# A two-layer diffusion trunk on one core: where PSUM changes hands around the MLPs, and a first stage that prepares two tiles ahead

## The chip, the cores and the metric

One core of a Trainium2 chip runs the whole program. The metric is the device time of one execution in microseconds; the kernel before took 1693.77 us in the median of three runs (1693.08 to 1694.43).

## What is computed

640 rows (512 latent, 128 context) of width 1024 pass two layers. Each has a mixer (differential attention, then neighbourhood attention) and a squared-ReLU MLP of width 4096; each half scales and shifts its input, multiplies its output by a gate and ends in a LayerNorm. Shift, scale and gate are columns of a modulation product. All in fp32.

```python
def modulate(x, shift, scale):
    return x * (1 + scale) + shift

def sq_relu_mlp(h, w1, w2):
    return jnp.square(jax.nn.relu(h @ w1)) @ w2

for i in range(DEPTH):
    mp = modulation(c_ctx, w_mod[i], b_mod[i])
    ...
    y, state = ctx_mixers[m](modulate(xp, mp[0], mp[1]), *params[i])
    xp = layer_norm(ALPHA * xp + mp[2] * y, ln_g[i, 0], ln_b[i, 0])
    y = sq_relu_mlp(modulate(xp, mp[3], mp[4]), w_mlp1[i], w_mlp2[i])
    xp = layer_norm(ALPHA * xp + mp[5] * y, ln_g[i, 1], ln_b[i, 1])
    ... # the same for the latent rows xs
```

## The kernel before

Every fp32 product is made of three matmuls: each operand is split into a high part (a cast, `hhi`, `wh`, `uhi`) and a low part (the difference, `hlo`, `wl`, `ulo`), and `mm3` (lines 120 to 122) adds high x high, low x high and high x low. So TensorE does three passes, ScalarE makes the high parts (L127 for activations, L195 for weights) and VectorE the low ones (L128, L197); with `pool_lo` above zero some low parts of weights go to GpSimd instead. Raw weights `rw` come through SP's DMA queue.

TensorE's instructions run in the order in which the program is written; the order on ScalarE, VectorE, GpSimd and SP is a scheduler's. PSUM has eight banks. `banks(kind, m)` closes the pools in use and opens others: two S tiles or O tiles in up to four banks, and `m` banks for M tiles (128 x 512). A tile of a new pool takes banks of the old one, so its first matmul waits until the old tile there has been read.

The places that the change touches, in order of time:

- `start` (0 to 57 us). Per tile of 128 input columns: modulation matmuls (L260), a copy and a transposition (L269), `mod_affine` (VectorE: `red`, `mc`, `AB`), scaling of `x` (L417), split, and `main`, 15 matmuls of 512 columns. Preparation of tile g stands around `main(g - 1)`.
- `rest` (the MLP of layer l; 443 to 905 us and 1247 us to the end). The up projection comes in four groups `gr` of two chunks c with four tiles f each. In group 0, chunk 0, the columns up to 256 were multiplied earlier (`first`, in S and O tiles); `act` squares them (ScalarE relu L1198, VectorE L1199, split L127 and L128), then `banks(None, 6)`, then the four tiles' columns from 256 on (M tiles of 384 columns). `act_ctx` squares the 128 context rows as `rc`, which are transposed on TensorE (L1217) after the next tile. `next(mods)` puts a step of the next layer's modulation columns on VectorE (L294, `jk`).
- The last down projection (`down`). For layer 0 `banks("S", 4)` stands ahead of it. Then, by `ORDER_LN`, n (down projection of a row tile, second half, with LayerNorm L1010 to L1020), h (transposition of the tile to h, L1060) and v (first value columns of layer 1) follow each other.

## Time and profile before

| | |
|---|---|
| median of 3 runs | 1693.77 us (1693.08 to 1694.43) |
| the profiled execution | 1694.21 us |
| its span | 1692.4 us |
| TensorE busy | 1611.3 us, 95% |
| VectorE, ScalarE, GpSimd busy | 65%, 40%, 19% |
| DMA, mean over the span | 119 GB/s |

Times in the rows are microseconds from the span's start. A matmul's duration in a row overlaps the next one's; how fast they follow is read from their starts. In brackets at a row's end stands how long the engine was idle before it, and which instruction it then waited for.

### The profile page before, as it was taken

Reading aid. Unit: us, or ns where it says so; the run is one execution under the profiler, and the core shown is the slowest. Engines: PE = TensorE matmul, PEld = TensorE weight load, DVE = VectorE, ACT = ScalarE, POOL = GpSimd, SP = SyncE. Lnnn points to the kernel's source line nnn. Section 1 sums busy time; section 2 is a strip of 40 time slices with the busy share of each in tenths; the row PEclk is TensorE's granted clock in tenths of the full one; section 3 lists DMA queues with packets and bytes.
Section 4 is the critical chain, followed back from the end, with each engine's and each line's share of the span. In section 5 each row is a group of like instructions: output and inputs, shape, how many; then the busy total and the mean of one; then the engine's idle time right before and its main releaser. Section 6 shows DMA issues by size and latency. Waiting matters only on the chain. (4 is left out here: it accounts for less than half of the span.)

```text
span 1692.4 us, 23972 instructions
## 1 busy us (share of the span) xinstructions
PE 1611.3 (95%) x9074; PEld 1394.7 (82%) x9074; DVE 1098.9 (65%) x2169; ACT 669.0 (40%) x1366; POOL 316.4 (19%) x260
## 2 busy tenths in 40 slices
PE   8999999899799999999999999998889999999997
PEld 5788889787788788778788999997788888888886
DVE  4788778875569979796365777778655543232337
ACT  2456555743531322312235555565452132131321
POOL 2100000000002236254211001100000224334321
PEclk9999999999899999999999999999999999999999
DMA  8442334331334545452224443444033122221211
GB/s 336 130 136 91 102 116 151 103 129 52 124 113 137 199 149 187 162 172 103 75 75 161 126 127 119 148 140 165 14 112 113 63 99 75 76 98 51 100 51 63
DMA packets 61367, 200.62 MB, mean 119 GB/s; under 512 B 7765, under 2 KB 14403, under 8 KB 60227
## 3 DMA queue, kind: packets, MB, share of 16 engines
q1 hardware_dynamic: 55618, 175.09, 30.3%
q0 software_dynamic: 5632, 23.99, 4.1%
q8 instruction: 72, 1.18, 0.3%
q14 instruction: 45, 0.36, 0.1%
HBM read 186.41 MB, written 7.40 MB: 115 GB/s over the span
## 5 line engine op out<-in xcount | busy, mean ns | idle before, releaser
L195 ACT CAST wh<-rw 128x1024 fp32r<-128x1024 f32 x192 | 200.2, 1053 | 380.1 <-PE M L122 287.9
L197 DVE TENSOR_TENSOR wl<-rw,wh 128x512 fp32r<-128x512 f32 x278 | 216.1, 811 | 128.7 <-ACT wh L195 128.0
L120 PE MATMUL M<-hhi,wh 128*128 128x512 f32 (+2 forms) x768 | 279.0, 363 | 8.1 <-DVE r L1199 7.9
L122 PE MATMUL M<-hhi,wl 128*128 128x512 f32 (+2 forms) x768 | 277.5, 361 | 1.8 <-DVE wl L197 1.8
L121 PE MATMUL M<-hlo,wh 128*128 128x512 f32 (+2 forms) x768 | 277.1, 361 | 0.0
L120 PE MATMUL M<-wh,uhi 128*128 128x512 f32 x640 | 250.9, 392 | 3.1 <-DVE rc L1199 3.1
L120 PE MATMUL M<-wh,hhi 128*128 128x256 f32 (+1 forms) x752 | 244.6, 325 | 8.7 <-DVE tmp L1143 3.2
L122 PE MATMUL M<-wh,ulo 128*128 128x512 f32 x640 | 249.9, 391 | 1.6 <-DVE ulo L128 1.6
L121 PE MATMUL M<-wl,uhi 128*128 128x512 f32 x640 | 249.9, 390 | 0.0
L197 POOL TENSOR_TENSOR wl<-rw,wh 128x512 fp32r<-128x512 f32 x106 | 181.9, 1726 | 345.0 <-ACT wh L195 344.7
L122 PE MATMUL M<-wh,hlo 128*128 128x256 f32 (+1 forms) x752 | 240.1, 319 | 5.0 <-DVE hlo L128 5.0
L121 PE MATMUL M<-wl,hhi 128*128 128x256 f32 (+1 forms) x752 | 239.5, 319 | 0.0
L120 PEld LDWEIGHTS M<-hhi,wh 128*128 128x128 f32 x768 | 146.1, 190 | 26.1 <-issue 8.2
L122 PEld LDWEIGHTS M<-hhi,wl 128*128 128x128 f32 x768 | 145.9, 190 | 20.8 <-DVE wl L197 3.3
L120 PEld LDWEIGHTS M<-wh,hhi 128*128 128x128 f32 x752 | 145.2, 193 | 20.6 <-DVE tmp L1143 3.4
L121 PEld LDWEIGHTS M<-hlo,wh 128*128 128x128 f32 x768 | 146.0, 190 | 17.2
L122 PEld LDWEIGHTS M<-wh,hlo 128*128 128x128 f32 x752 | 144.8, 193 | 17.9 <-DVE hlo L128 9.1
L121 PEld LDWEIGHTS M<-wl,hhi 128*128 128x128 f32 x752 | 145.2, 193 | 8.7
L120 PEld LDWEIGHTS M<-wh,uhi 128*128 128x128 f32 x640 | 120.5, 188 | 28.3 <-issue 3.5
L294 DVE SCALAR_TENSOR_TENSOR jk<-wm,cb 128x1024 bf16<-128x1024 f32 x96 | 141.7, 1476 | 2.9 <-DMA wm<-in_wmodT 1.9
L122 PEld LDWEIGHTS M<-wh,ulo 128*128 128x128 f32 x640 | 120.6, 188 | 27.7 <-DVE ulo L128 2.4
L121 PEld LDWEIGHTS M<-wl,uhi 128*128 128x128 f32 x640 | 120.6, 188 | 25.1 <-DVE wl L197 0.4
(284 smaller groups left out, 2459.9 us busy)
## 6 DMA issues: line engine op xcount, KB each, us to landing
rw<-in_w SPq DMA_DIRECT2D x192, 512.0 KB, 3.8
wm<-in_wmodT SPq DMA_DIRECT2D x48, 512.0 KB, 3.5
rw<-in_wmod SPq DMA_DIRECT2D x32, 512.0 KB, 4.5
E<-in_bias POOLq DMA_DIRECT2D x32, 384.0 KB, 5.2
wm<-in_wmod SPq DMA_DIRECT2D x8, 1024.0 KB, 10.8
Q<-Q SPq DMA_DIRECT2D x16, 320.0 KB, 3.8
gate<-gates POOLq DMA_DIRECT2D x6, 512.0 KB, 5.1
X<-in_xT SPq DMA_DIRECT2D x8, 320.0 KB, 11.4
```

Source lines behind the costliest of these rows:

```text
L120: te.matmul(out, sh, mh, start=start, stop=False)
L121: te.matmul(out, sh, ml, start=False, stop=False)
L122: te.matmul(out, sl, mh, start=False, stop=stop)
L195: keep(nc.scalar.copy(hi, r))
L197: keep(eng.tensor_tensor(lo[:, k], r[:, k], hi[:, k], ALU.subtract))
L294: op = nc.vector.scalar_tensor_tensor(jk, ws[t], 1.0, cb[:, x, :], ALU.mult, ALU.mult, accum_out=mc[:, t, x : x + 1])
```

## The change

Four edits. (1) `start` loads three tiles ahead, does the modulation, scaling and split of two tiles ahead of the first `main`, then two rounds ahead, and `pool_lo` is 0, so that VectorE makes all low parts. (2) In the MLP, `banks(None, 6)` moves from ahead of the first chunk to behind it; in layer 1 a `banks("S", 4)` stands ahead of the chunk. `banks("S", 4)` ahead of the last down projection of layer 0 is gone, and v takes M tiles, two to a bank. (3) `next(mods)` moves from `square` to `aside`, behind the split, and no longer follows the context squares; the transpositions of the context rows come after the second tile of a chunk. (4) `ORDER_LN` has v0 ahead of h3 and v2 ahead of h4.

```diff
-ORDER_LN = "n0 n1 h0 n2 h1 n3 h2 n4 h3 v0 v1 h4 v2 v3"
+ORDER_LN = "n0 n1 h0 n2 h1 n3 h2 n4 v0 h3 v1 v2 h4 v3"
...
-        self.pool_lo = 2
+        self.pool_lo = 0
...
+            for g in range(3):
+                load(g)
+            mod(0)
+            self.conv(0, False)
+            affine(0)
+            mod(1)
+            affine(1)
+            for g in range(KT - 1):
+                load(g + 3)
+                main(g, (0, 1))
+                if g == 0:
+                    main(g, (2, 3, 4))
+                mod(g + 2)
+                if g % 2:
+                    self.conv(g // 2 + 1, False)
...
+                if g:
+                    main(g, (2, 3, 4))
+                affine(g + 2)
             main(KT - 1, range(NTT))
...
             def square(r, src):
                 nc.scalar.activation(r, src, AF.Relu)
-                op = nc.vector.scalar_tensor_tensor(r, src, 0.0, r, ALU.max, ALU.mult)
-                if not quiet:
-                    next(mods, None)
-                return op
+                return nc.vector.scalar_tensor_tensor(r, src, 0.0, r, ALU.max, ALU.mult)
...
-            def aside(op):
+            def aside(op, x=0):
+                if gr and x < 2:
+                    next(mods, None)
...
                             act(us, f, first[f], slice(0, CUT))
-                        self.banks(None, 6)
+                        if l == 1:
+                            self.banks("S", 4)
                         for f in range(4):
                             m = self.M()[:, : NT - CUT]
                             self.ff(n, f, CUT, NT, m)
                             act(us, f, m, slice(CUT, NT))
+                        self.banks(None, 6)
...
                         aside(act(us, 4 * c + f, m, slice(0, NL)))
-                        while wait:
-                            wait.pop()()
+                    while wait:
+                        wait.pop()()
...
                 if t % 2 == 0:
-                    box.append(self.S())
-                m = box[-1][:, 512 * (t % 2) :]
-                self.nat(hT, t, NCH, m[:, :256], 0, 256)
+                    box.append(self.M())
+                m = box[-1][:, 256 * (t % 2) : 256 * (t % 2) + 256]
+                self.nat(hT, t, NCH, m, 0, 256)
...
             g, b = self.ln_tiles(pool, l, 1)
-            if l == 0:
-                self.banks("S", 4)
```

The functions `load`, `mod` and `affine` hold what stood in the loop of `start`: the DMA of a tile's weights and inputs (the first tile's weights in two halves); the modulation matmuls and the copy of their rows; the transposition, `mod_affine`, the scaling and the split.

TensorE at the entry of the first MLP, before: the last matmul of another S tile, the first of the first chunk (M_5274), the last of the fourth (M_5364), and the tile that follows (M_5431).

```order
L122 MATMUL S_5093<-hhi,wl_4998 128x256
L120 MATMUL M_5274<-hhi,wh_4831 128x384 [waits DVE_49,PE_49]
...
L122 MATMUL M_5364<-hhi,wl_4998 128x384
L120 MATMUL M_5431<-hhi,wh_5034 128x512
L121 MATMUL M_5431<-hlo,wh_5034 128x512
```

The same place in the changed kernel (M_5265, M_5355, M_5427), and the first matmul of the same chunk in the second MLP (M_12365).

```order
L122 MATMUL S_5089<-hhi,wl_4994 128x256
L120 MATMUL M_5265<-hhi,wh_4827 128x384 [waits Activation_49]
L121 MATMUL M_5265<-hlo,wh_4827 128x384 [waits DVE_49]
...
L122 MATMUL M_5355<-hhi,wl_4994 128x384
L120 MATMUL M_5427<-hhi,wh_5030 128x512 [waits DVE_49]
...
L120 MATMUL M_12365<-hhi,wh_12093 128x384 [waits DVE_49,PE_49]
```

The wait for VectorE (in both kernels for a square of a tile that held the bank) has moved from the first chunk to the tile behind the fourth; the first chunk waits only for the high and low parts of the last h tile. In the second MLP the first chunk waits for a square as before, and so does the tile behind its fourth.

VectorE in the third group of the first MLP, before: the square of the fourth tile (r_7017), two products of the modulation columns (jk), the low part of the square (ulo) and the square of the context rows (rc).

```order
L1199 SCALAR_TENSOR_TENSOR r_7017<-M_6917,r_7017 128x512 [waits Activation_49]
L294 SCALAR_TENSOR_TENSOR jk_7020,mc_103<-wm_6912,cb 128x1024 [waits DMAHW1_49,DVE_49]
L197 TENSOR_TENSOR wl_7035<-rw_6942,wh_7034 128x512 [waits DMAHW2_49,Activation_49]
L294 SCALAR_TENSOR_TENSOR jk_7022,mc_103<-wm_6912,cb 128x1024 [waits DVE_49]
L128 TENSOR_TENSOR ulo_6843<-r_7017,uhi_6842 128x512 [waits Activation_49]
L1199 SCALAR_TENSOR_TENSOR rc_7041<-M_6918,rc_7041 128x512 [waits Activation_49]
```

The same place in the changed kernel.

```order
L1218 SCALAR_TENSOR_TENSOR r_7001<-M_6901,r_7001 128x512 [waits Activation_49]
L197 TENSOR_TENSOR wl_7019<-rw_6926,wh_7018 128x512 [waits DMAHW1_49,Activation_49]
L128 TENSOR_TENSOR ulo_6827<-r_7001,uhi_6826 128x512 [waits Activation_49]
L294 SCALAR_TENSOR_TENSOR jk_7006,mc_103<-wm_6898,cb 128x1024 [waits DMAHW0_49]
L1218 SCALAR_TENSOR_TENSOR rc_7025<-M_6902,rc_7025 128x512 [waits Activation_49]
L294 SCALAR_TENSOR_TENSOR jk_7008,mc_103<-wm_6898,cb 128x1024 [waits DVE_49]
```

The products have moved behind the low part, the second of them behind the context square too.

TensorE from the end of layer 0 into layer 1, before: the last of v1 (in S_8533), h4's transpositions (L1060), the first of v2 (S_8606), the last of v3, and the first q/k matmul of layer 1 (M_8686).

```order
L122 MATMUL S_8533<-wh_8477,hlo 128x256
L1060 MATMUL M_8582<-idf,X_4337 128x128 [waits DVE_49,Pool_49]
...
L120 MATMUL S_8606<-wh_8213,hhi 128x256
...
L122 MATMUL S_8606<-wh_8477,hlo 128x256
L120 MATMUL M_8686<-hhi,wh_8213 128x320 [waits PE_49,Activation_49]
L121 MATMUL M_8686<-hlo,wh_8213 128x320 [waits DVE_49]
```

The same place in the changed kernel (v2 and v3 in M_8571, q/k in M_8674).

```order
L122 MATMUL M_8571<-wh_8466,hlo 128x256
L1081 MATMUL M_8596<-idf,X_4333 128x128 [waits DVE_49,Pool_49]
...
L120 MATMUL M_8571<-wh_8202,hhi 128x256 [waits Activation_49]
...
L122 MATMUL M_8571<-wh_8466,hlo 128x256
L120 MATMUL M_8674<-hhi,wh_8202 128x320 [waits DVE_49,PE_49]
```

One v more stands ahead of h4's transpositions, one less behind; the v's are M tiles, and the first q/k matmul waits for VectorE, for the split of a v whose bank it takes.

## Rows read from the trace of the kernel before

**Rows 1.** The page's first part: busy time, share of the span and instructions.
```profile
PE 1611.3 (95%) x9074; PEld 1394.7 (82%) x9074; DVE 1098.9 (65%) x2169; ACT 669.0 (40%) x1366; POOL 316.4 (19%) x260
```

**Rows 2.** TensorE's waits: for whom, us in total, times, longest.
```profile
PE M L120 <- DVE r L1199: 7.9, 2, 4.3
...
PE S L120 <- ACT hhi L127: 4.3, 5, 1.2
...
PE M L1060 <- DVE X L1020: 3.7, 1, 3.7
...
PE M L120 <- DVE rc L1199: 3.1, 1, 3.1
...
PE M L1217 <- DVE rc L1199: 2.3, 2, 1.2
PE M L120 <- DVE red L271: 2.2, 1, 2.2
...
PE M L122 <- DVE ulo L128: 1.6, 2, 0.8
```

**Rows 3.** Stretches: length, busy (PE, PEld, DVE, ACT, POOL), granted clock, DMA share, GB/s.
```profile
447.00:453.80 6.80, 5.89 (x18) 5.92 (x19) 2.72 (x7) 2.14 (x6) 2.28 (x5) 0.50 1.00 347
540.00:740.00 200.00, 194.60 (x860) 159.31 (x859) 175.98 (x234) 53.26 (x68) 76.01 (x42) 1.00 0.50 171
836.10:839.50 3.40, 3.40 (x10) 2.62 (x9) 0.00 (x0) 0.00 (x0) 0.00 (x0) 0.50 0.47 154
900.00:917.00 17.00, 13.30 (x87) 13.13 (x87) 8.69 (x16) 7.41 (x19) 4.10 (x8) 0.80 0.50 180
904.40:911.20 6.80, 5.71 (x27) 5.74 (x28) 2.12 (x3) 4.04 (x10) 0.00 (x0) 0.50 0.39 148
960.00:985.00 25.00, 20.79 (x154) 20.03 (x153) 20.78 (x58) 17.65 (x44) 4.05 (x8) 1.00 0.47 156
1249.10:1256.00 6.90, 5.83 (x18) 5.87 (x19) 1.20 (x4) 0.84 (x3) 0.00 (x0) 0.51 0.70 259
```

**Rows 4.** First stage: VectorE and GpSimd in time, then 20 to 57 us.
```profile
17.53 0.17 DVE L332 TENSOR_SCALAR AB<-mc 128x2 f32<-128x2 f32 x1
...
23.03 1.22 DVE L332 TENSOR_SCALAR AB<-mc 128x2 f32<-128x2 f32 x1
...
21.68 2.54 POOL L197 TENSOR_TENSOR wl<-rw,wh 128x512 fp32r<-128x512 f32 x2 [8.82 <-ACT wh L195]
...
20.00:57.00 37.00, 33.48 (x205) 22.55 (x202) 21.82 (x46) 13.35 (x22) 10.18 (x8) 1.00 0.62 239
```

**Rows 5.** Entry of the first MLP, in time: start, us, engine, what.
```profile
443.14 0.69 DVE L128 TENSOR_TENSOR hlo<-hs,hhi 128x512 fp32r<-128x512 f32 x1 [1.57 <-ACT hhi L127]
...
447.91 0.66 PE L120 MATMUL M<-hhi,wh 128*128 128x384 f32 x1 [4.30 <-DVE r L1199]
...
467.35 0.39 PE L120 MATMUL M<-hhi,wh 128*128 128x512 f32 x1
```

**Rows 6.** The fourth chunk's square: ScalarE, then VectorE, in time.
```profile
467.61 0.49 ACT L1198 ACTIVATE r<-M 128x384 f32<-128x384 f32 x1
...
466.41 3.09 DVE L197 TENSOR_TENSOR wl<-rw,wh 128x512 fp32r<-128x512 f32 x5
469.43 0.55 DVE L1199 SCALAR_TENSOR_TENSOR r<-M,r 128x384 f32<-128x384 f32 x1
```

**Rows 7.** Third group of the first MLP: VectorE's product, TensorE's wait.
```profile
724.36 1.21 DVE L294 SCALAR_TENSOR_TENSOR jk<-wm,cb 128x1024 bf16<-128x1024 f32 x1
...
726.24 0.50 PE L122 MATMUL M<-wh,ulo 128*128 128x512 f32 x1 [0.79 <-DVE ulo L128]
```

**Rows 8.** Layer 1's start: first q/k matmul, last split of V.
```profile
914.72 0.31 PE L120 MATMUL M<-hhi,wh 128*128 128x320 f32 x1
...
916.19 0.42 DVE L128 TENSOR_TENSOR V<-S,V 128x256 fp32r<-128x256 f32 x1 [0.44 <-ACT V L127]
```

**Rows 9.** The fourth chunk's square in the second MLP.
```profile
1271.65 0.55 DVE L1199 SCALAR_TENSOR_TENSOR r<-M,r 128x384 f32<-128x384 f32 x1
```

More of the change, by code (lines that the diff above doesn't have):

```diff
@@ L384, in start, with load @@
                 nc.tensor.matmul(warm[:, :P], self.idf, self.ones, start=True, stop=True)
-            for g in range(KT):
-                w = pool.tile([P, 2, 4, 256], F32, tag="wm0", name=self.nm("wm"), bufs=4)
-                nc.sync.dma_start(w, a["wmod"][g])
-                nc.sync.dma_start(x[:, g, :], a["xT"][:, g, :])
-                if g % 2 == 0:
-                    self.pump()
-                acc = self.M()
-                self.mod_mm(acc, w[:, 0], 0)
-                self.mod_mm(acc, w[:, 1], 1)
-                rows = pool.tile([P, 256], F32, tag="rows", name=self.nm("rows"), bufs=2)
-                self.tc.keep_in_program_order(nc.scalar.copy(rows, acc[:, :256]))
-                if g % 2 == 0:
-                    self.conv(g // 2, False)
+            ws, rows = {}, {}
+            def load(g):
+                if g < KT:
+                    ws[g] = pool.tile([P, 2, 4, 256], F32, tag="wm0", name=self.nm("wm"), bufs=4)
+                    for r in (slice(0, 1), slice(1, 2)) if g == 0 else (slice(0, 2),):
+                        nc.sync.dma_start(ws[g][:, r], a["wmod"][g][:, r])
+                    if g == 2:
+                        self.pump()
+                    nc.sync.dma_start(x[:, g, :], a["xT"][:, g, :])
+                    if g == 0 or g == 4 or g == 6:
+                        self.pump()
                 if g == KT - 1:
@@ L404, in start, with mod, affine @@
                     nc.sync.dma_start(self.bm[1], a["bmodT"][1])
+            def mod(g):
+                if g < KT:
+                    acc = self.M()
+                    self.mod_mm(acc, ws[g][:, 0], 0)
+                    self.mod_mm(acc, ws[g][:, 1], 1)
+                    rows[g] = pool.tile([P, 256], F32, tag="rows", name=self.nm("rows"), bufs=2)
+                    self.tc.keep_in_program_order(nc.scalar.copy(rows[g], acc[:, :256]))
+            def affine(g):
+                if g < KT:
+                    self.mod_T(rows[g], g)
+                    self.mod_affine(0, 0, g)
+                    for t, c in enumerate((slice(0, NL), slice(NL, NT))):
+                        nc.vector.tensor_scalar(
+                            x[:, g, c], x[:, g, c], A[:, 0, g, t : t + 1], mc[:, g, t : t + 1], ALU.mult, ALU.add
+                        )
+                    self.split(h[0][:, g, :], h[1][:, g, :], x[:, g, :])
+            for g in range(3):
[13 more added lines that the diff above has]
+                    self.conv(g // 2 + 1, False)
+                if g == KT - 2:
                     self.pin = True
@@ L407, in start @@
                     self.ready += 1
-                if g > 0:
-                    main(g - 1, (0, 1))
-                self.mod_T(rows, g)
-                if g > 0:
-                    main(g - 1, (2, 3, 4))
-                self.mod_affine(0, 0, g)
-                cuts = (0, 256, NL, NT) if g == KT - 1 else (0, NL, NT)
-                for c0, c1 in zip(cuts, cuts[1:]):
-                    t, c = c0 // NL, slice(c0, c1)
-                    nc.vector.tensor_scalar(
-                        x[:, g, c], x[:, g, c], A[:, 0, g, t : t + 1], mc[:, g, t : t + 1], ALU.mult, ALU.add
-                    )
-                    if g == KT - 1:
-                        self.split(h[0][:, g, c], h[1][:, g, c], x[:, g, c])
-                if g < KT - 1:
-                    self.split(h[0][:, g, :], h[1][:, g, :], x[:, g, :])
+                if g:
+                    main(g, (2, 3, 4))
+                affine(g + 2)
             main(KT - 1, range(NTT))
@@ L1250, in rest @@
                         continue
-                    quiet = gr == 0
                     for f in range(2):
@@ L1264, in rest @@
                         if k == 3:
-                            aside(act(us, 4 * c + 2 + x, ms[x], slice(0, NL)) if x < 2 else act_ctx(us, c, ms[x]))
+                            aside(act(us, 4 * c + 2 + x, ms[x], slice(0, NL)) if x < 2 else act_ctx(us, c, ms[x]), x)
                 if gr < 3:
```

1 line of the change is left out of this document (removed).

## The prediction, made before the changed kernel had run

> **What bounds the kernel now.** I read the page's first part first: TensorE is busy for 1611.3 of 1692.4 us and VectorE for 65% of it [rows 1]. TensorE is the bound, its work is not changed by one matmul, and so the change can only be worth what TensorE waits, and what it runs slowly after waiting. Next the list of its waits, longest in total first [rows 2]: it is a list of single events with a place each, and six of the seven lines shown belong to places that the diff touches. Last the granted clock by stretches [rows 3]: behind each wait of over 3 us that matters here the clock stands at 0.50, which is the lower of its two levels (1.2 GHz of 2.4), while 540 to 740, with two waits of 0.8 and two of 1.2 us in it, has 1.00 on the whole. A stretch of 3.4 us at half speed puts TensorE back by 1.7 us; so a wait that goes is worth itself plus half of the slow stretch behind it, and a wait that comes costs the same. The profiled execution took 1694.21 us, 1.8 us more than its span and 0.4 us more than the median of 1693.77 us; the sum is made against 1694.2 and 0.4 is taken off at the end.
>
> **First stage.** Its loop works tile by tile: modulation matmuls, a transposition, scaling on VectorE, a split, 15 matmuls. Every second round GpSimd makes two low parts (2.54 us) beside VectorE's scaling, and a tiny operation of VectorE, 0.17 us alone, then takes 1.22 us [rows 4]; TensorE waits for the split, five times in all, 4.3 us [rows 2]. The change prepares two tiles ahead and gives the low parts to VectorE. TensorE has 33.48 us of work between 20 and 57 us, so 3.5 us is idle there [rows 4]. With a lead of a whole round (about 4.5 us) over a chain of some 3 us, I count that idle as gone: **+3.5 us**. VectorE takes over the low parts, at 0.62 us each (five in 3.09 us, [rows 6]), 1.24 us a pair against GpSimd's 2.54; it is busy for 21.8 of those 37 us [rows 4], so there is room. The bounds: the five waits and the smaller ones give at most 5; if the first main matmuls come later, because the second tile's modulation now stands ahead of them, 1. The loads are issued three tiles ahead on SP's queue; their sum is the same, and what they push back are weights of the next chunk, needed only after 50 us.
>
> **Entry of the first MLP.** The first four chunks (columns from 256, 96 matmuls) get their bank today from the squares of the 256-column part: TensorE stands for 4.30 us until 447.91 [rows 5] and then runs at half speed to 453.8. In the changed kernel the first chunk writes a bank of the old pool. What it waits for is the last h tile: its low part is ready at 443.83 [rows 5], the second half of it before TensorE gets there. Start at 443.9 instead of 447.9 is 4.0, and 5.9 us at half speed, no longer there, is 2.9: **+6.9 us**. But the new pool now opens directly behind the fourth chunk, and the matmul that follows takes bank 2, which holds until VectorE has squared a tile of the fourth chunk. Today nobody waits for that: TensorE goes on at 467.35 [rows 5], ScalarE's relu of the chunk comes at 467.61, since two casts stand ahead of it, VectorE's square at 469.43, behind five low parts (3.09 us), and is done at 469.98 [rows 6]. The order of both engines there is the same after the change. So TensorE stands from the chunk's end, 467.4 in today's time, to about 469.9: **-2.5 us**. Behind that wait stand the whole second half of the first group's up projection. Net +4.4; bounds +1 (with 6.8 us at half speed behind the wait, as at 447) and +6.9 (if the square comes early).
>
> **Does the clock fall behind 2.5 us?** The rows leave it open: waits of 3.1 and more were followed by a fall, waits of up to 1.2 were not [rows 2, 3]. There will be two such waits (the second MLP has the other), and I count one fall of 3.4 us: **-1.7 us**. The Trainium skill, page TensorE: Matmul & The Clock Gate, section "A second HAM failure mode: psum-queue depth-cycling", says that short idles between groups, where a kernel cycles through PSUM banks, can be enough to make the clock swing. By that both waits would bring a fall and the sum would be 1.7 us less; the stretch from 540 to 740, which has such short idles at 1.00 [rows 3], speaks against it.
>
> **Middle of the first MLP.** VectorE computes the modulation columns of the next layer (1.21 us a product, [rows 7]) between a square and its low part; twice TensorE waits 0.79 us for that low part [rows 7], in all 1.6 us [rows 2]. The new order has the low part ahead of the product: gone. The transpositions of the context rows come after the second tile instead of the first; they wait 1.17 us twice today (2.3 us, [rows 2]) for a square that is queued behind products on VectorE. A tile is 24 matmuls of 0.23 us (860 in 194.6 us, [rows 3]), 5.5 us of cover: gone. **+3.9 us** together. The products that no longer follow the context squares move into the last group; VectorE is busy for 176 of 200 us in the middle [rows 3], so a new short wait of about a microsecond is possible; bounds +2 and +3.9.
>
> **Last down projection of the first MLP.** Today the pools are closed and opened ahead of it, so its first matmul waits for the square of the last context tile, 3.1 us [rows 2], and 3.4 us at half speed follow [rows 3]. The switch is removed; the tile takes the next of six banks, long free. **+4.7 us** (3.1 and 1.7, less 0.1). In the second MLP, which has no switch there, the list shows no such wait. Bounds +3 and +4.8.
>
> **End of layer 0.** v0 now stands ahead of h3 and v2 ahead of h4. So the 3.70 us that h4's transpositions wait for the LayerNorm [rows 2], until about 905.4, are filled with v2 (24 matmuls, half as wide, of 0.12 us, 2.9 us), and h4 comes at the same time, at full clock. But the v tiles have left the S banks for the M pool, and when layer 1 opens its own M pool, the first q/k matmul takes a bank whose v must have been split. Today it starts at 914.72, directly behind v3, while VectorE splits the last v until 916.61 [rows 8]: the changed kernel makes TensorE wait for just that. ScalarE and VectorE still do the five v's behind h4's own casts. I put that end at 914.5 (2 us earlier, as h4 and v3 don't run at half speed any more), v3's end at 909: the wait has moved from before h4 to behind v3 and grown to 5.5 us. Start of q/k: 0.2 us earlier than now; 3.4 to 6.8 us at half speed behind it cost 1.7 to 3.4. **-2 us**; bounds +5.6 (the v's are split in time, TensorE goes on at 909) and -5 (the splits are no earlier than now, and the long slow stretch).
>
> **Entry of the second MLP.** The same edit does something else here: a pool is opened ahead of the first chunk after all (the S banks and four M banks), and the chunk still takes the bank of a 256-column tile and waits for its square, as the order of the instructions shows; its wait (3.6 of the 7.9 us, [rows 2]) and the slow stretch [rows 3] stay. The new wait behind the fourth chunk comes too: that square runs from 1271.65 to 1272.20 [rows 9], 16.2 us after the slow stretch of that entry ends at 1256.0, as the first one ends 16.2 us after 453.8, so I take the same price. **-2.5 us**; bounds -5.9 (with the long slow stretch) and 0.
>
> **Sum**: 3.5 + 4.4 + 3.9 + 4.7 - 2.0 - 2.5 - 1.7 = 10.3 us; 1694.2 - 10.3 - 0.4 gives **1683.5 us**. The two terms least certain, the first stage (1 to 5) and the clock behind the three new waits (none to three falls of 1.7 beyond what is counted), move it by about 4.5 either way: 1679 to 1688.
>
> **Rivals.**
> - *The banks come free in time* at the q/k start and behind the fourth chunks. For: with TensorE earlier by some microseconds, the casts ahead of the relu could run before the chunk ends. Against: in the new order what TensorE waits for is the fourth chunk's square and the last v split. Then 3.5 + 6.9 + 3.9 + 4.7 + 5.6 + 0 = 24.6: 1669; with half of it 1676.
> - *Long slow stretches behind all three new waits*, 6.8 us each as at 447 and 904 [rows 3]: 3.5 + 1.0 + 3.9 + 4.7 - 3.4 - 5.9 = 3.8: 1690.
> - *The first stage's gain is taken back* by the next wait, the 2.2 us for a reduction on VectorE near 99 us [rows 2], as VectorE has no less to do: 6.8 left, 1687.
> - *Slower: hand-over after hand-over in layer 1's start.* The M pool there has four banks, now filled in step with late splits; if TensorE pauses at each of them, the clock could stay near the 0.80 that it has from 900 to 917 [rows 3] for the 71 us to 985. That costs 0.2 x 71 = 14 us, and with the sum of 10.3 gives -3.9: 1697.5. It decides there: the kernel is slower than before from a mean clock under 0.85 (0.15 x 71 = 10.6), measurably so from about 0.80. By that section of the page TensorE: Matmul & The Clock Gate of the Trainium skill this would be the expected course. The trace bears it out nowhere: 960 to 985, with several short waits in 25 us of which TensorE works 20.8, has 1.00 [rows 3].
>
> **How the numbers follow.** 0.2%, 3.4 us, is about what a measurement of this kernel tells from no change. Likeliest case 0.62 (1679 to 1688), banks free 0.09 (1669 to 1678), long slow stretches 0.12 (1688 to 1692), first stage given back 0.11 (1685 to 1689), slower 0.06 (above 1697). Faster means under 1690.4: 0.62 + 0.09 + 0.11 + half of 0.12 is 0.87 with rounding down for what I haven't seen; slower 0.05, same 0.08. The range from 1675 to 1690.5 leaves out most of the first rival, half of the second and the last, under 2 in 10.
>
> **What would show it.** In the changed trace: no wait for squares at 444 and a clock of 1.00 from 444 to 460; a wait of about 2.5 us for a square one chunk group later, and again some 800 us later; the waits for the context squares and the low parts gone from the list; the last down projection without a wait; h4 without one, but the first q/k matmul waiting 5 us for a split of V; the square at the second MLP's entry waiting 3.6 us as now. The forecast is wrong if the q/k start doesn't wait, if the wait at the fourth chunk is absent, or if the first stage still ends near 56 us.

## The result, and the profile after

The changed kernel takes 1681.07 us (median of 4 runs, 1680.45 to 1681.81) against 1694.1 us for the kernel before beside it (4 runs, 1693.08 to 1694.43): a ratio of 0.9931, 95% interval 0.9919 to 0.9944, or 13 us less. The forecast was 1683.5 us, with a range from 1675 to 1690.5: right, and 2.4 us too high. The profiled execution of the changed kernel took 1680.74 us, 13.5 us less than the profiled one of before (its span is 1678.7 us, 13.7 less); the sum of the forecast, made against that one, was 10.3.

The first part of the page of the changed kernel, which answers to [rows 1]:

```profile
span 1678.7 us, 23945 instructions
PE 1608.3 (96%) x9074; PEld 1395.9 (83%) x9074; DVE 1099.7 (66%) x2176; ACT 668.9 (40%) x1364; POOL 307.7 (18%) x250
```

TensorE issues the same 9074 matmuls and is busy for 3.0 us less; the other 10.7 us of the shorter span are waits. The list of its waits (for whom, us in total, times, longest), which answers to [rows 2]; line numbers have moved, L1199 of before is L1218:

```profile
PE M L120 <- DVE r L1218: 8.5, 3, 3.4
...
PE M L120 <- DVE V L128: 5.4, 1, 5.4
...
PE M L120 <- DVE red L271: 2.2, 1, 2.2
```

Gone are the five waits of the first stage for hhi, the 3.7 for the LayerNorm, the 3.1 and the 2.3 for context squares, and the 1.6 for low parts. New is the 5.4 for a split of V. The squares of a chunk (r) are still waited for, three times instead of two. The stretches that answer to [rows 3] and the last line of [rows 4] (length, busy time of PE, PEld, DVE, ACT and POOL, granted clock, DMA share, GB/s):

```profile
20.00:57.00 37.00, 36.84 (x241) 27.84 (x242) 23.94 (x61) 16.11 (x27) 0.00 (x0) 1.00 0.73 275
440.00:456.50 16.50, 16.38 (x95) 16.29 (x95) 8.41 (x19) 9.27 (x20) 3.12 (x6) 1.00 0.67 256
456.90:463.70 6.80, 4.29 (x13) 3.33 (x13) 4.37 (x8) 2.21 (x4) 0.00 (x0) 0.75 0.72 235
540.00:740.00 200.00, 198.41 (x882) 163.58 (x881) 168.28 (x217) 55.47 (x71) 86.20 (x46) 1.00 0.48 163
892.40:904.40 12.00, 6.55 (x27) 6.51 (x27) 2.54 (x6) 2.78 (x8) 4.10 (x8) 0.72 0.64 218
1231.80:1238.60 6.80, 3.38 (x12) 3.33 (x12) 2.99 (x8) 2.49 (x7) 2.08 (x4) 0.75 0.79 288
```

In 37 us of the first stage TensorE now does 241 matmuls where it did 205, in 200 us of the middle 882 where it did 860. The entry of the first MLP runs at full clock; the two new waits stand at 457 and at 892, each with a piece at half speed.

**Where the 13 us are.** Both programs have 9074 matmuls, and from one place to the next the k-th of the one can be set beside the k-th of the other. The difference of their starts, before less after, is what the changed kernel has gained up to there. The last column has the parts in a second trace of the changed kernel, which is told of below:

```
up to (time before)            gained   in this part   forecast     second trace
end of the first stage, 73      4.56        +4.6         +3.5            +3.8
entry of the first MLP, 435     3.69        -0.9          -               0.0
  first chunk, 456             10.55        +6.9         +6.9            +6.9
  behind the fourth chunk, 475  6.20        -4.3         -2.5 -1.7       -4.4
its middle, 821                11.97        +5.8         +3.9            +5.9
its last down projection, 848  16.99        +5.0         +4.7            +5.0
q and k of layer 1, 921        14.00        -3.0         -2.0            -1.5
entry of the second MLP, 1250  14.87        +0.9          -              +1.2
end, 1681                      13.35        -1.5         -2.5            -4.1
```

Whether TensorE's clock falls behind one of its waits of 2 to 4 us differs between runs of the same kernel (a table of it stands at the end). So a part's worth is read below from such starts in the two traces at that place, and whole times, which hold a handful of such falls, are given beside it.

### The profile page after: what moved, and what is told of

Its sections match the earlier page's. It is cut to its first block, busy times and chain, and to the rows that moved or that the text cites. A ratio compares the mean times of both kernels' runs of the same rounds, so it can differ in the third digit from the quotient of the medians.

```text
span 1678.7 us, 23945 instructions
## 1 busy us (share of the span) xinstructions
PE 1608.3 (96%) x9074; PEld 1395.9 (83%) x9074; DVE 1099.7 (66%) x2176; ACT 668.9 (40%) x1364; POOL 307.7 (18%) x250
## 4 chain that ended last, share of the span: by engine, by line
PE 77%; DVE 11%; issue 5%; ACT 4%; DMA 3%; POOL 0%; DVEq 0%; SPq 0%; ACTq 0%; POOLq 0%
PE M L120 22%; PE M L122 22%; PE M L121 22%; DVE wl L197 3%; PE S L482 1%; PE S L483 1%; PE M L260 1%; PE S L120 1%; DMA rw<-in_w 1%; PE S L121 1%; PE S L122 1%; DVE jk L294 1%; PE M L618 1%; ACT wh L195 1%; ACT hs L1084 1%
## 5 line engine op out<-in xcount | busy, mean ns | idle before, releaser
L197 DVE TENSOR_TENSOR wl<-rw,wh 128x512 fp32r<-128x512 f32 x288 | 221.4, 804 | 124.2 <-ACT wh L195 123.4
L120 PE MATMUL M<-hhi,wh 128*128 128x512 f32 (+2 forms) x768 | 279.6, 364 | 14.1 <-DVE r L1218 8.5
L120 PE MATMUL M<-wh,hhi 128*128 128x256 f32 (+1 forms) x784 | 254.4, 324 | 7.7 <-DVE tmp L1164 3.2
L122 PE MATMUL M<-wh,hlo 128*128 128x256 f32 (+1 forms) x784 | 249.7, 318 | 5.1 <-DVE hlo L128 5.1
L120 PE MATMUL M<-wh,uhi 128*128 128x512 f32 x640 | 250.1, 391 | 0.0
L121 PE MATMUL M<-wl,hhi 128*128 128x256 f32 (+1 forms) x784 | 249.3, 318 | 0.0
L197 POOL TENSOR_TENSOR wl<-rw,wh 128x512 fp32r<-128x512 f32 x96 | 171.7, 1798 | 302.8 <-ACT wh L195 302.7
L120 PEld LDWEIGHTS M<-hhi,wh 128*128 128x128 f32 x768 | 146.1, 190 | 32.9 <-issue 9.2
L120 PEld LDWEIGHTS M<-wh,hhi 128*128 128x128 f32 x784 | 152.1, 194 | 19.1 <-DVE tmp L1164 3.4
L122 PEld LDWEIGHTS M<-wh,hlo 128*128 128x128 f32 x784 | 151.5, 193 | 17.9 <-DVE hlo L128 9.2
L121 PEld LDWEIGHTS M<-wl,hhi 128*128 128x128 f32 x784 | 152.1, 194 | 9.5 <-DVE wl L197 0.7
L294 DVE SCALAR_TENSOR_TENSOR jk<-wm,cb 128x1024 bf16<-128x1024 f32 x96 | 145.8, 1519 | 1.0
L120 PEld LDWEIGHTS M<-wh,uhi 128*128 128x128 f32 x640 | 120.1, 188 | 24.5
```

What stands on the lines that cost most here:

```text
L120: te.matmul(out, sh, mh, start=start, stop=False)
L121: te.matmul(out, sh, ml, start=False, stop=False)
L122: te.matmul(out, sl, mh, start=False, stop=stop)
L197: keep(eng.tensor_tensor(lo[:, k], r[:, k], hi[:, k], ALU.subtract))
L294: op = nc.vector.scalar_tensor_tensor(jk, ws[t], 1.0, cb[:, x, :], ALU.mult, ALU.mult, accum_out=mc[:, t, x : x + 1])
```

## The experiments

Twelve kernels were run, in three groups; the kernel before took 1692.5, 1692.3 and 1692.7 us beside them. Each is the changed kernel with the edit shown, but for one that is the changed kernel again.

**The first stage as it was** (the old loop, and two low parts of each pair given to GpSimd).

```
-        self.pool_lo = 0
+        self.pool_lo = 2
...
-            for g in range(3):
-                load(g)
-            mod(0)
-            self.conv(0, False)
-            affine(0)
-            mod(1)
-            affine(1)
-            for g in range(KT - 1):
-                load(g + 3)
-                main(g, (0, 1))
...
+            for g in range(KT):
+                w = pool.tile([P, 2, 4, 256], F32, tag="wm0", name=self.nm("wm"), bufs=4)
+                nc.sync.dma_start(w, a["wmod"][g])
...
+                if g > 0:
+                    main(g - 1, (0, 1))
```

> The changed kernel with the first stage of before. Theory (the stage itself gives 4.6 us in the trace, and 1.4 us of it go back to a slow stretch behind the 2.2 us wait at 95 us, which the old stage doesn't have): 3.2 to 3.6 us more than the changed kernel's 1681.1, so 1684.5 us; the wait comes near 99.8 us with a clock of 1.00 behind it. Rival (the gain is given back by later waits on VectorE): within 1 us of 1681.

Measured: 1685.88 us, ratio to before 0.9954 (0.9939 to 0.9969). The wait `PE S L120 <- ACT hhi L127: 4.3, 5, 1.1` is back; the 425th matmul starts 5.7 us later than in the changed kernel's first trace. The whole time is 4.8 us more. The first stage is worth what its waits say, and a little more. One part of what I expected failed: the clock does fall here behind the wait for red (at 101.5 us), which it did not do in the trace of before.

**The lead of two tiles kept, GpSimd back.** My forecast put the gain of the first stage down to the lead, and took VectorE's extra work as affordable. This tells the two apart.

```
-        self.pool_lo = 0
+        self.pool_lo = 2
```

> In the first stage GpSimd makes two low parts of a weight tile again, as before; the lead of two tiles stays. My forecast's reading (the lead covers the stretched operations of VectorE): the stage's end within 1 us of the changed kernel, 1681 to 1682 us. Rival (the gain came from taking GpSimd away from VectorE's side): the five waits are back, 3 to 4.5 us more, 1684.5 to 1686 us.

Measured: 1687.85 us, ratio 0.9969 (0.9957 to 0.9981). My reading fails: nearly the whole gain of the stage is gone. The list of TensorE's waits and the stretch from 20 to 57 us of this kernel:

```profile
PE M L269 <- ACT rows L411: 0.5, 1, 0.5
PE M L121 <- DVE wl L197: 0.3, 1, 0.3
PE M L120 <- ACT wh L195: 0.3, 1, 0.3
PE M L260 <- DMA rw<-in_wmod: 0.3, 1, 0.3
20.00:57.00 37.00, 36.09 (x228) 25.67 (x225) 21.39 (x47) 13.41 (x22) 10.58 (x8) 1.00 0.66 246
```

The rival's picture fails as well: the five waits do not come back. The lead hides them, and the 300th matmul starts at 54.5 us, where it starts at 52.5 in the changed kernel and at 57.3 before. The rest is lost by another way. GpSimd, VectorE, SyncE's queue and ScalarE of this kernel, in time:

```profile
25.10 2.53 POOL L197 TENSOR_TENSOR wl<-rw,wh 128x512 fp32r<-128x512 f32 x2 [12.19 <-ACT wh L195]
26.35 1.30 DVE L276 TENSOR_TENSOR mc<-red,bm 128x4 f32<-128x4 f32 x1
...
50.83 3.00 POOL L197 TENSOR_TENSOR wl<-rw,wh 128x512 fp32r<-128x512 f32 x2 [2.85 <-ACT wh L195]
53.85 0.91 SPq L183 DMA_DIRECT2D rw<-in_w  x2
57.49 1.05 ACT L195 CAST wh<-rw 128x1024 fp32r<-128x1024 f32 x1 [2.63 <-DMA rw<-in_w]
```

and SyncE's queue and ScalarE at the same place of the changed kernel:

```profile
49.79 1.53 SPq L183 DMA_DIRECT2D rw<-in_w  x2
55.78 1.05 ACT L195 CAST wh<-rw 128x1024 fp32r<-128x1024 f32 x1 [1.00 <-DMA rw<-in_w]
```

GpSimd reads the raw weight tiles (rw) until 53.83, and the next loads into such tiles are issued at 53.85, 4 us later than in the changed kernel (49.79); the cast is later, and TensorE runs into weights that are not ready behind the stage: from the 300th to the 425th matmul the kernel loses another 2.2 us. At the 425th it stands at 72.3 us: 0.3 us before the kernel before, 4.2 behind the changed one. The lead and the low parts on VectorE are worth 4.6 together, and the lead alone 0.3. Traces of the same stage differ by 1 to 2 us here: the eleven with the whole new stage have the 425th matmul at 67.2 to 69.1 us, the two with the old one at 72.7 and 73.8, so the lead alone gives 0.3 against the one and 1.5 against the other. The low parts on VectorE without the lead were not run; what they would give alone is not shown.

**The middle of the first MLP as it was** (products behind the squares, context transposes behind the first tile).

```
+            quiet = True
...
+                if not quiet:
+                    next(mods, None)
...
-                if gr and x < 2:
-                    next(mods, None)
...
+                    quiet = gr == 0
...
-                    while wait:
-                        wait.pop()()
+                        while wait:
+                            wait.pop()()
```

> The changed kernel with the modulation products and the context transpositions where they were before. Theory A (a wait of TensorE is worth its idle time alone, 1.17 twice and 0.79 twice): 3.9 us more, 1685.0 us. Theory B (the ledger between the two traces: each wait is worth 0.2 to 0.3 us more than its idle time, and two short waits for low parts of weights come with it): 5.8 us more, 1686.9 us.

Measured: 1686.79 us, ratio 0.9962 (0.9948 to 0.9976). Between 408 and 774 us the difference of its starts to the changed kernel's goes from -1.4 to 4.2, by 5.6: theory B. The waits from 540 to 800 us of this kernel and the stretch that answers to the one above:

```profile
PE M L1238 <- DVE rc L1220: 2.3, 2, 1.2
PE M L122 <- DVE wl L197: 1.9, 3, 1.1
PE M L122 <- DVE ulo L128: 1.6, 2, 0.8
535.00:735.00 200.00, 194.45 (x860) 159.19 (x859) 175.39 (x232) 53.27 (x68) 75.82 (x42) 1.00 0.53 170
```

It has 22 matmuls less in 200 us, 5.0 us at 0.227 each, while the idle time differs by 4.0: the first matmul behind a wait is itself longer (0.50 us in [rows 7], 0.39 in a running stream), and a wait costs 0.2 to 0.3 us more than it is long.

**The hand-over in the MLPs as it was** (all banks switched ahead of the first chunk, in both).

```
-                        if l == 1:
-                            self.banks("S", 4)
+                        self.banks(None, 6)
...
-                        self.banks(None, 6)
```

> The changed kernel with the PSUM hand-over ahead of the first chunk in both MLPs, as before. Theory (first MLP gains 2.6 us net by the move, second loses 0.5): 2.1 us more than the changed kernel, 1683.2 us; the waits for squares are 4.3 and 3.6 us at the two entries, none behind the fourth chunks. Rival (the wait behind the fourth chunk gives back all that the entry gains): 1681.

Measured: 1679.63 us, ratio 0.9918 (0.9898 to 0.9937): no slower than the changed kernel. By places: at the first MLP's entry the wait is back, `PE M L120 <- DVE r L1218: 4.3, 1, 4.3`, and 6.5 us are lost; behind its fourth chunk there is no wait and 4.4 come back. In the second MLP there is no wait behind the fourth chunk either, which gives 2.8 against the first trace of the changed kernel and 4.4 against the second, in which the clock fell behind that wait. So this edit of the change gains 2.1 us in the one MLP and loses 2.8 to 4.4 in the other (the forecast's terms were 2.7 and -2.5): over both it is worth nothing at best.

**The clock behind the fourth chunk.** Eleven matmuls without use are put into the wait, into a free tile.

```
+                        idle = self.S()
+                        for _ in range(11):
+                            nc.tensor.matmul(idle[:, :NL], hT[0][:, 0, :P], hT[0][:, 0, :NL], start=True, stop=True)
```

> Eleven matmuls without use are put into the wait behind the fourth chunk of each MLP, into a free S tile; the wait for the square keeps its length. Theory (the slow stretch comes from TensorE standing there): no half-speed stretch behind that place in either MLP, 1.8 us less in the first and up to 1.8 in the second, 1678 to 1680 us. Rival (the stretch comes from the load on the chip, not from the standing): stretch as before, 1681 to 1682 us.

Measured: 1676.87 us, ratio 0.9899 (0.9883 to 0.9916). The added matmuls in the first MLP, the next one of the program behind them, and the stretches behind the place in both MLPs:

```profile
457.28 2.70 PE L1269 MATMUL S<-hhi 128*128 128x512 f32 x11
459.96 0.50 PE L120 MATMUL M<-hhi,wh 128*128 128x512 f32 x1
459.90:463.30 3.40, 3.40 (x16) 2.77 (x16) 1.86 (x4) 1.56 (x2) 0.00 (x0) 1.00 0.83 305
1252.00:1255.40 3.40, 3.40 (x16) 2.63 (x15) 2.03 (x4) 1.52 (x2) 0.00 (x0) 1.00 0.78 284
```

The same first stretch of the changed kernel:

```profile
459.50:462.90 3.40, 3.40 (x10) 2.66 (x11) 1.85 (x3) 1.51 (x2) 0.00 (x0) 0.61 0.87 288
```

The square comes as late as before (458.87 us in the changed kernel, 459.4 here, in a trace 0.5 us behind), but the clock stays at its upper level, and 16 matmuls go where 10 went. By starts the kernel gains 1.6 us at that place, the forecast's price for one fall, and 1.6 in the second MLP against the trace in which the clock fell there too; the rest of the 4 us that it is ahead are falls elsewhere. The half-speed stretch comes from TensorE standing, not from what the other engines do.

**Two extra banks as a pool of their own**: the four M banks in use go on, and the two S banks, long free, become a second pool, which takes every third M tile, so that no pool is opened over banks that have just been closed.

```
-                        if l == 1:
-                            self.banks("S", 4)
...
-                        self.banks(None, 6)
+                        self.more()
...
+    def more(self):
+        self.psB[1].close()
+        self.psS = self.psS[:1]
+        self.psB = None
+        st = ExitStack()
+        self.psX = (st.enter_context(self.psum(self.nm("psX"), 2)), st)
```

> The two extra M banks come as a second pool beside the six-bank layout instead of a reopening of all banks, in both MLPs, so that no tile waits for the last tile of the old pools. Theory (the hand-over waits are the reopening's): the wait of 2.51 us in the first MLP's fourth chunk with its half-speed stretch goes (4.35 us), and in the second MLP the entry wait of 3.4 us with its stretch (about 4.6) and the fourth chunk's of 2.5: about 11.7 us, 1669.4 us. Rival (the matmuls meet the relu and its reads at the next bank, so the waits only move): 1677 to 1681 us.

Measured: 1669.46 us, ratio 0.9856 (0.9829 to 0.9883), against 1681.69 of the unedited changed kernel beside it. The waits for squares are gone from the list, in both MLPs. Two stretches of this kernel, the first MLP's first group, and the second's:

```profile
425.00:475.00 50.00, 48.59 (x287) 45.36 (x288) 31.29 (x56) 27.39 (x59) 3.13 (x6) 0.97 0.40 144
1224.60:1261.00 36.40, 36.40 (x199) 33.95 (x198) 18.64 (x32) 16.09 (x31) 2.10 (x4) 0.97 0.34 116
```

In the second TensorE doesn't stop at all. In the first the fourth chunk's square comes as late as before (461.09 us, in a trace that is 2.2 us behind there), and nobody waits for it; of the 1.4 us of idle time 1.3 are a wait at 430. By starts to the unedited kernel beside it 4.4 us are gained in the first MLP and 10.6 from the entry of the second on (7.7 against the first trace of the changed kernel, whose clock fell less there); falls of the clock behind the wait for red and just ahead of the second MLP take 3.3 back. The theory holds. In the compiled changed kernel the matmul behind the fourth chunk writes bank 2, while the square that it waits for reads bank 5 (2 and 3 in the second MLP): it had no need of that square, and the reopening made it wait for the tile released last, whichever bank it got. The forecast took this wait as a cost of the new order, with bank 2 held by the square, and the section on the change says the same of the tile that held the bank; it is a cost of the way in which the banks are handed over.

**The changed kernel again**, as the measure for the kernels run beside it.

> The changed kernel unedited, as the measure for the three kernels beside it on the same chip: 1681 us. If the places where TensorE's clock falls behind waits of 2 to 4 us are the same as in the first profile, they are set by the program; if they differ, single differences of 1 to 3 us between whole times are not to be read as the price of an edit.

Measured: 1681.69 us, ratio 0.9936 (0.9918 to 0.9955). From 90 to 900 us the waits of over 1.5 us are the same within 0.2; behind three that both have, the clock behaves otherwise, and by starts the two traces drift apart by up to 4.8 us and end 0.6 apart. The stretch behind the wait for red, 2.24 us in both, in the first trace and in this one:

```profile
95.20:98.60 3.40, 3.39 (x16) 3.39 (x17) 3.40 (x7) 2.16 (x4) 0.00 (x0) 0.53 0.79 254
96.00:99.40 3.40, 3.39 (x28) 3.39 (x29) 3.40 (x7) 2.21 (x4) 0.00 (x0) 1.00 0.86 240
```

The 1.4 us that the first stage's gain of 4.6 lost by the 650th matmul are this fall, and no property of the change: in the second trace the stage gained 3.8 and lost nothing there.

**The end of layer 0 as it was**, and, in another kernel, its banks alone (the new order of V and LayerNorm stays). The order, in the first alone:

```
-ORDER_LN = "n0 n1 h0 n2 h1 n3 h2 n4 v0 h3 v1 v2 h4 v3"
+ORDER_LN = "n0 n1 h0 n2 h1 n3 h2 n4 h3 v0 v1 h4 v2 v3"
```

The banks, in both:

```
-                    box.append(self.M())
-                m = box[-1][:, 256 * (t % 2) : 256 * (t % 2) + 256]
+                    box.append(self.S())
+                m = box[-1][:, 512 * (t % 2) :]
...
+            if l == 0:
+                self.banks("S", 4)
```

> The changed kernel with the end of layer 0 of before: pools switched ahead of the last down projection, v in S tiles, the old order of n, h and v. Theory (the switch costs 5.0 us, the wait at the first q/k matmul 2.8 us more than the one ahead of h4): 2.2 us more, 1683.3 us. Rival (the wait at the q/k start costs what its idle time and slow stretch are, 8.6 us, against 3.70 and 3.4 for h4, so the end of layer 0 loses as much as the switch gives): 1681.

> Only the banks at the end of layer 0 as before (the V chunks in S banks, the pools switched ahead of the last down projection); the new order of V chunks and LayerNorm stays. By my forecast's terms the switch costs its wait of 3.1 us with or without a slow stretch (3.3 to 4.7 us), and the q and k matmuls don't wait (5.5 us and about 2.5 for the clock gained): about 1678 us. Rival (with the V chunks in S banks the next matmul of the S pool or the first scores waits for the same late splits): 1681 to 1684 us.

Measured: 1680.51 us (ratio 0.9928, 0.9904 to 0.9951) and 1681.22 us (0.9926, 0.9904 to 0.9947): neither differs from the changed kernel. The waits of the two between 815 and 920 us, the first kernel's two rows ahead:

```profile
PE M L1081 <- DVE X L1041: 3.7, 1, 3.7
PE M L120 <- DVE rc L1218: 3.1, 1, 3.1
...
PE M L120 <- DVE rc L1218: 3.1, 1, 3.1
PE M L120 <- ACT wh L195: 1.1, 1, 1.1
```

The wait at the last down projection costs 3.4 us in both (behind it the clock does not fall here, as it did in the trace of before), and the q and k matmuls start without one. But in the first kernel h4 waits 3.7 us ahead of them, as before, and the second, some 15 us behind their start, meets weights that are not cast, with a half-speed stretch (919.4 to 922.8 at 0.53), and gives 3.8 back. What the change gains at the last down projection it pays at the start of layer 1: behind these places the kernels with the old banks are 0.6 to 0.9 us ahead of the changed kernel's first trace and as much behind its second. In the pair of traces of the table above the two places gave 2.0, since there a fall of the clock went with the old wait. My forecast's 2.7 for the two holds for that pair alone; on the second kernel the rival's time came, and not the 1678 of my terms, though TensorE met weight casts further on and not, as the rival had it, late splits.

**Why q and k wait for V.** The chain at that place of the changed kernel, in time:

```profile
888.42 0.33 SPq L1042 DMA_DIRECT2D x<-X  x1
893.24 0.33 SPq L500 DMA_DIRECT2D X<-in_cv  x1
893.31 0.69 DVE L128 TENSOR_TENSOR hlo<-hs,hhi 128x512 fp32r<-128x512 f32 x1 [1.02 <-ACT hhi L127]
895.38 0.40 ACT L127 CAST V<-X 128x256 fp32r<-128x256 f32 x1 [2.10 <-DMA X<-in_cv]
896.16 1.61 DVE L128 TENSOR_TENSOR V<-M,V 128x256 fp32r<-128x256 f32 x4
897.92 0.60 PE L120 MATMUL M<-hhi,wh 128*128 128x320 f32 x1 [5.45 <-DVE V L128]
```

My forecast had the V casts queued behind h4's own. Those are done by 893.3, and ScalarE then stands for 2.1 us: the first cast in its queue is the cached V of layer 1, whose load is issued at 893.24, 4.8 us behind the write of a tile of x1 (888.42), into a buffer of those from which x1 is written. Two kernels test this: one loads and casts the cached V and K of the pair behind the pair's own, the other puts the four V chunks into one S tile, so that the q and k matmuls take no bank of theirs.

```
-            cr = self.io(pool)
-            self.nc.sync.dma_start(cr, self.a[cache][:, 256 * i : 256 * i + 256])
-            put(4, cr)
+            def cached():
+                cr = self.io(pool)
+                self.nc.sync.dma_start(cr, self.a[cache][:, 256 * i : 256 * i + 256])
+                put(4, cr)
...
+        if i == 0 and not hf:
+            self.cached_v()
+            self.cached_k(pool, self.a["ck1T"][i], K[:, :, 256:384])
```

> The cached V and K of layer 1's first pair are loaded and cast behind the pair's own V and K, nothing else changed. Theory (the V casts queue on ScalarE behind the cached V, whose load waits for the X tile that the write of x1 frees): q and k start about 2.2 us earlier, at about 895.5 instead of 897.9, about 1678.7 us. Rival, my forecast's own reading (the wait is the queue of h4's casts and splits): q and k start where they did, 1681 us.

```
-                if t % 2 == 0:
-                    box.append(self.M())
-                m = box[-1][:, 256 * (t % 2) : 256 * (t % 2) + 256]
+                if t == 0:
+                    box.append(self.S())
+                m = box[-1][:, 256 * t : 256 * t + 256]
```

> All four V chunks of layer 1's first pair go into one S tile, so that the q and k matmuls no longer take a bank that waits for a V split; the V splits themselves stay late behind the cached V's DMA. Theory (that bank is the whole wait): the 5.45 us wait before q and k goes with the half-speed stretch behind it, 8.6 us in all, about 1672.5 us. Rival (q, k or the first scores meet the same late splits a little further on): 1676 to 1681 us.

Measured: 1679.45 us (0.9921, 0.9901 to 0.9940) and 1678.83 us (0.9915, 0.9898 to 0.9931), 2.2 and 2.9 less than the changed kernel beside them; the intervals overlap, and the rows decide. In the first:

```profile
895.45 0.65 ACT L127 CAST V<-M 128x256 fp32r<-128x256 f32 x2 [0.80 <-DVE hlo L128]
897.62 0.48 PE L120 MATMUL M<-hhi,wh 128*128 128x320 f32 x1 [3.78 <-DVE V L128]
```

The wait is 3.78 instead of 5.45 us. Of the 2.2 us expected 1.7 are there; now the V casts wait for h4's last low part, as my forecast had it. Both causes are real, and the cached V was the later. In the second the wait is gone and q and k start 6.4 us earlier, but 18 us on TensorE waits 0.9 us for a weight cast, and a half-speed stretch follows (911.7 to 915.1 at 0.57): 3.6 are given back, 2.8 stay. The cast stands behind the cached K, which is late like the cached V:

```profile
907.74 0.41 ACT L474 CAST K<-X 128x256 fp32r<-128x256 f32 x1 [5.92 <-DMA X<-in_ck1T]
909.22 1.04 ACT L195 CAST wh<-rw 128x1024 fp32r<-128x1024 f32 x1
```

Theory and rival each have a part.

**All three edits together** (extra banks, V in one S tile, cached V and K later).

> The three earlier edits together: the two extra M banks as a second pool, the four V chunks in one S tile, the cached V and K of layer 1 behind the pair's own. Theory (the three waits are independent): 12.2 us from the banks, 2.9 from the S tile and up to 2.2 from the cached load, about 1665 us. Rival (the clock falls elsewhere for it, so that the parts don't add): 1669 us, as with the banks alone.

Measured: 1663.65 us (1662.06 to 1667.48), ratio to before 0.9827 (0.9807 to 0.9847). The parts add in the whole times: 12.2, 2.9 and 2.2 from 1681.7 make 1664.4. By starts the two edits at q and k give 3.7 us together, 2.8 of which the S tile gives alone. It is the best of the kernels and takes 29 us off the kernel before.

## Why the prediction was right, point by point

- **First stage, +3.5 forecast, 4.6 measured.** The size was right to the bounds, the reason half wrong, and so the size is in part luck. I counted the idle time as covered by the lead, and took VectorE's extra work for a side effect that fits. The lead alone is worth 0.3 to 1.5 us; without GpSimd's low parts out of the way the next chunk's loads and casts come late. I compared the two engines' durations and did not ask what holds the buffers into which SyncE loads next; about half of the 4.2 us is lost that way, behind the stage.
- **Entry of the first MLP, +6.9 and -2.5 -1.7 forecast, 6.9 and -4.3 measured.** Both terms hit. The order of the instructions had shown which square the next tile would wait for, and the durations in [rows 6] gave the end. The reason that I gave, a bank held by that square, is wrong: the square reads bank 5, and the tile takes bank 2. The rows of the changed kernel:

```profile
455.86 3.09 DVE L197 TENSOR_TENSOR wl<-rw,wh 128x512 fp32r<-128x512 f32 x5
457.06 0.49 ACT L1217 ACTIVATE r<-M 128x384 f32<-128x384 f32 x1
458.87 0.55 DVE L1218 SCALAR_TENSOR_TENSOR r<-M,r 128x384 f32<-128x384 f32 x1
459.47 0.50 PE L120 MATMUL M<-hhi,wh 128*128 128x512 f32 x1 [2.52 <-DVE r L1218]
```

- **The clock behind the two new waits, one fall forecast.** In the first trace it was one of two. Over the nine traces that have both waits it fell nine times in the first MLP and seven in the second. Two falls would have been the better count. My premise was wrong as well: I wrote that waits of up to 1.2 us were not followed by a fall. The trace of before has a fall that I overlooked, behind idles of 0.45 and 1.07 us with ten small matmuls between them, and it is in all fourteen traces:

```profile
215.39 1.28 PE L632 MATMUL M<-mean,sq 128*128 128x1 f32 x10 [0.45 <-ACT X L622]
217.74 0.83 PE L597 MATMUL M<-idf,E 128*128 128x128 f32 x5 [1.07 <-DVE V L128]
218.30:221.70 3.40, 3.06 (x15) 2.82 (x14) 2.71 (x7) 1.70 (x3) 0.00 (x0) 0.50 0.76 258
```

  The Trainium skill, page TensorE: Matmul & The Clock Gate, section "A second HAM failure mode: psum-queue depth-cycling", by which I gave two falls as the other case, was nearer than I was, for waits of 2.5 us and, by these rows and the falls at 912 and 919 above, for some of about 1 us. For the idles of 0.8 and 1.2 us in the middle, which I set against it, the rows agree with me (535 to 735 us of the kernel with the old middle, at 1.00).
- **Middle, +3.9 forecast, 5.8 measured.** The term that was mis-sized most. I summed idle times; each wait costs 0.2 to 0.3 us more, and two short waits for weights' low parts, which cost 0.3 and 0.6 us, went too. The new waits that I had in the bound did not come, VectorE being busy for 168 of 200 us instead of 176.
- **Last down projection, +4.7 forecast, 5.0 measured** in that pair of traces; 3.4 where the old wait is not followed by a fall. The forecast's lower bound of 3 was the other of the two cases.
- **End of layer 0, -2.0 forecast, -3.0 measured.** The wait was foreseen with its place and length (5.5 against 5.45 us), by a chain of which a link was wrong: the cached V, not h4's casts, comes last. In the second trace, whose slow stretch there is half as long, the part is -1.5.
- **Second MLP, -2.5 forecast, -1.5 measured.** Wait at the entry as before (3.42 us against 3.59), the new one of 2.52 behind the fourth chunk. In the first trace the slow stretch at the entry was half as long as in [rows 3], which gave 1.2 back, and the clock did not fall behind the fourth chunk. In the second trace it fell, and the part is -4.1; the forecast lies between the two.
- **The rivals.** The banks did not come free in time. The long stretches of 6.8 us came behind q and k alone. The first stage's gain was not taken back at the wait for red. Nor did the clock stay low in layer 1's start:

```profile
897.90:969.00 71.10, 68.22 (x467) 67.50 (x468) 43.16 (x115) 36.96 (x87) 5.95 (x13) 0.93 0.40 129
```

The errors of the terms are +1.1, -0.2, +1.9, +0.3, -1.0 and +1.0, and the parts without a term cancel (-0.9 and +0.9): 3.1 in sum. The 0.4 that I took off for the median of before, and the 0.3 by which the median of the changed kernel stands above its profiled execution, leave the 2.4. With the parts of the second trace the total is 12.7, and other errors cancel: how near the sum came is in part luck of the clock. Of the errors of a microsecond and more only the middle's stands in both.

## What to carry to other kernels

When PSUM banks are regrouped, ask which release the first tile of the new pool waits for: here it was the last one of all banks closed, and a second pool beside the old one was worth 12 us, as much as all the rest of the change. Price a wait at its length plus 0.2 to 0.3 us, and add a fall of the clock (1.6 us here) that may or may not come, mostly from 2.2 us on but in places behind idles of about 1 us; so compare parts by the starts of the same instruction in two traces, not by whole times. When an operation is moved from one engine to another, look at what its old engine held: here about half of the gain lay in the weight tiles that came free earlier.

## What the runs showed of the hardware

**The clock behind a wait differs from run to run.** Granted clock in the 4 us behind the same wait, over the fourteen traces (before, changed, and the twelve kernels), counted where the wait is there:

```
wait, us          place                       traces   clock fell
0.45, 1.07        near 215                      14       14
0.89, 0.16, 0.23  weight cast, near 910          1        1
1.07, 0.17, 0.22  weight cast, near 917          1        1
1.70, 1.57        near 1135                     14        0
2.04              near 402                      14        4
2.24              for red, near 95               14        8
2.52              fourth chunk, first MLP         9        9
2.52              fourth chunk, second MLP        9        7
3.13              last down projection            3        1
3.16              second attention, near 1204    14       11
3.0 and 3.2       near 330 and 423               14       14 each
```

One fall puts TensorE back by 1.4 to 1.8 us. The same program at the same place can go either way, and neither the length of the wait nor the place alone decides it: idles of 1.07 us near 215 are followed by a fall in every trace, waits of 1.70 us near 1135 in none.

**Small operations of VectorE beside GpSimd.** In the rows of the kernel with GpSimd back in the first stage, an operation of 128x4 elements runs from 26.35 to 27.65 us, to the end of GpSimd's second low part (25.10 plus 2.53). The same operation in the changed kernel, whose GpSimd rests from 20 to 57 us (group of instructions: count, busy us, mean ns, idle before):

```profile
L276 DVE TENSOR_TENSOR mc<-red,bm 128x4 f32<-128x4 f32 x6 | 1.0, 164 | 0.2
```

The 1.22 us of [rows 4] end in the same way at 24.25, GpSimd's pair at 24.22. The page SBUF — State Buffer of the Trainium skill, section "SBUF: two separate sides", has the two engines share a port pair that the one which starts first holds for its whole instruction; the rows agree.
